# Spreading modulation rows over the partitions with TensorE products, and moving small loads from ScalarE's queue to GpSimd's

## The chip, the cores and the metric

The kernel runs on one core of a Trainium2 chip. The metric is the device time of one execution in microseconds (us), the median over several runs; lower is better. A profile is one further execution, seen by the hardware profiler. In its rows PE is TensorE's matmul, PEld its weight load, DVE is VectorE, ACT is ScalarE, POOL is GpSimd, and SP is the sync engine, which does nothing here but issue DMAs. A name with a q behind it (ACTq, SPq) is the queue side of the engine: the issuing of a DMA, or a wait.

## The reference, cut to what matters

Two networks run one after the other on a sequence of 256 tokens of width 1024. The first has two layers, with a second stream of 256 context tokens (needed in layer 0 only). A layer takes six modulation vectors from a conditioning vector and uses two of them as gates on its two outputs:

```
mod = s_c @ ada_w[l] + ada_b[l]
sh1, sc1, g1, sh2, sc2, g2 = split(mod, 6)
hx = rms_norm(x, norm1_g[l]) * (1.0 + sc1) + sh1
y  = token_mixers(hx, ...) @ w_out          # four mixers: gating, Fourier, two attentions
x  = x + g1 * y
x  = x + g2 * expert_choice_ffn(rms_norm(x, norm2_g[l]) * (1.0 + sc2) + sh2, ...)   # 16 experts
```

`g1` and `g2` are one number for each of the 1024 columns, the same for all tokens. The context stream has its own modulation from the same weights. The second network has two layers of two recurrent mixers, a projection and a feed-forward part; the change doesn't touch its code.

## The kernel before

Tokens lie on the partitions (two tiles of 128 for a stream), the 1024 columns along the free axis. The kernel is written as a Python program whose order is not the order that runs: a scheduler simulates the program at build time and puts each engine's instructions in a fixed list, which the engine then works off strictly in order. An instruction that waits holds up all behind it on its engine. A DMA stands in the list of the engine that issues it.

In order of time, for each of the two layers of the first network:

- `Mods.one` works out a third of the modulation in eight steps: each step loads 1 MB of `ada_w` (SP) and multiplies it in (`pada`, L182). Before the first step the tile `ab` is zeroed on GpSimd (L169) and two loads put the bias `ada_b` into it (L171); after the last, DVE adds it (L187), which gives a row tile, `mrow`. A row tile has 128 partitions, of which eight carry something: partition 32j holds columns 512j to 512j+511 of the token stream's slice, partition 32j+1 the context stream's. Steps that aren't yet needed are put between other work.
- `G1.params` loads one tile of parameters (`pr`, L221) and one of gains (`gn`, L227), a small exponential (`lls`, L234) is made from the latter, and a transpose (`pp`, L223) from the former. In layer 0 it stands in the middle of the first eight modulation steps; the loads for layer 1 are issued in layer 0.
- `G1.hx` norms the tokens: sums of squares (`xn`, L272 on DVE and L274 on ACT), a short chain on DVE, a scaling (L291), transposes on PE (`pt`, L296), and modulation and split into a high and a low part (`hf`, `hT`, L298 to L301).
- The mixers: products with `w_in` (`tokgemm`; its weights `w` come by SP and are split into `whl` by ACT, L62, and DVE, L63; three products for each, L316 to L318), attention units (`psc`, `e`, `wT`), Fourier (`pf`), gating. `bias` is the table of the neighbourhood attention, loaded for each unit by SP.
- `merge` and `project`: the four outputs times `w_out`, times the gate `g1` (DVE, `wtmp`), added to x. The multiplication needs `g1` on all 128 partitions: `g1b`. Here a DMA on SP's queue reads the one partition of `mrow` that holds the row and writes it to 128 (L600): four such copies in layer 0, two in layer 1. The scheduler is free to issue them as soon as `mrow` exists.
- `moe`: `g2` is spread in the same way (L920, four copies to 32 partitions in layer 0, two to 64 in layer 1), then the router, and 16 experts' units whose weights (12 MB for an expert) come by SP in pieces of 1 MB.

PSUM tiles of `moe` and `project` come from pools that take the place of the mixers' pools. The pool `E.m` has one buffer during the mixers and four during `project` and `moe`.

Of the kernel before, what the change touches and what calls it, by code (L numbers as in the profile page):

```python
# [7 lines left out]
FT = mybir.dt.float32  # L8
FR = mybir.dt.float32r
I32 = mybir.dt.int32  # L10
AF = mybir.ActivationFunctionType
# [55 lines left out]
def pairs(r):  # L67

    return slice(256 * (r // 2) + r % 2, 256 * (r // 2) + 256, 2)
# [47 lines left out]
def raw(E, src, kn, st=False):  # L117

    pool, tag = (E.st, "st") if st else (E.wp, "w")
    w = pool.tile([128, kn, src.shape[1]], FT, name="w", tag=tag)  # L120
    E.nc.sync.dma_start(w, src.rearrange("(k p) n -> p k n", p=128))
    return w
# [13 lines left out]
class Mods:  # L136
# [28 lines left out]
    def one(self, l, r, k):  # L165
        E, nc, C = self.E, self.E.nc, self.E.c2
        if k == 0:
            self.ab = E.md.tile([128, 512], FT, name="ab", bufs=1)
            nc.gpsimd.memset(self.ab, 0.0)  # L169
            for s in range(2):  # L170
                nc.scalar.dma_start(self.ab[s:128:32], E.i["ada_b"][l, 2048 * r:2048 * r + 2048].rearrange("(j n) -> j n", j=4))  # L171
            self.ps = E.ad.tile([128, 512], FT, name="pada", tag="ada")
        src = E.i["ada_w"][l, 128 * k:128 * k + 128, 2048 * r:2048 * r + 2048]

        if (l, r) == (0, 0) and k < 3:
            w = E.hl.tile([128, 2048], FT, name="w", tag="whl")
            nc.sync.dma_start(w, src)
        else:
            w = raw(E, src, 1, (l, r) == (0, 0) and k < 7)[:, 0]
        ws = [w[:, 512 * j:512 * j + 512] for j in range(4)]  # L180
        for j in range(4):
            nc.tensor.matmul(self.ps[32 * j:32 * j + 32], self.st[:, k], ws[j],  # L182
                             start=(k == 0), stop=(k == KC - 1), skip_group_check=True)
        if k < KC - 1:
            return
        row = E.md.tile([128, 512], FT, name="mrow", bufs=2) if r else self.ab
        nc.vector.tensor_add(row, self.ps, self.ab)  # L187
        self.row[l, r] = row
        pt = E.m.tile([128, 4, 128], FT, name="pmt", tag="m")
        for q in range(4):  # L190

            nc.tensor.transpose(pt[:, q], row[:, pairs(q) if r else slice(128 * q, 128 * q + 128)], C.id)
        mt = E.md.tile([128, 4, 4, 2], FT, name=f"mt{r}", bufs=2)
        for s in range(2):
            nc.vector.tensor_copy(mt[:, :, :, s], pt[:, :, s:128:32].rearrange("p q j -> p j q"))
        self.T[l, r] = mt
# [7 lines left out]
class G1:  # L204
# [13 lines left out]
    def params(self):  # L218
        E, l, nc, C = self.E, self.l, self.E.nc, self.E.c2
        pr = E.md.tile([32, 128], FT, name="pr1", bufs=1)  # L220
        nc.scalar.dma_start(pr, E.i["par1"][l])  # L221
        pp = E.m.tile([128, 32], FT, name="pp1", tag="m")
        nc.tensor.transpose(pp, pr, C.id[0:32, 0:32])  # L223
        self.pc = E.md.tile([128, 32], FT, name="pc1", bufs=2)
        nc.vector.tensor_copy(self.pc, pp)
        g = E.md.tile([128, 256], FT, name="gn1", bufs=1)
        nc.scalar.dma_start(g, E.i["gains1"][l].unsqueeze(0).to_broadcast([128, 256]))  # L227

        lf = g[:, 128:256].rearrange("p (a b d) -> p a b d", a=2, b=2)
        pd = E.md.tile([128, 2, 32], FT, name="lpd", bufs=1)  # L230
        nc.vector.tensor_mul(pd, lf[:, :, 0], lf[:, :, 1])
        ls = E.md.tile([128, 2], FT, name="lls", bufs=1)
        nc.vector.tensor_reduce(ls, pd, axis=AX.X, op=OP.add)
        nc.scalar.activation(ls, ls, AF.Exp)  # L234
        self.nlam = E.md.tile([128, 1], FT, name="nlam", bufs=2)
        nc.vector.scalar_tensor_tensor(self.nlam, ls[:, 1:2], -self.lam_init, ls[:, 0:1], op0=OP.add, op1=OP.subtract)
        self.gdq = E.md.tile([128, 1], FT, name="gdq", bufs=2)
        nc.vector.tensor_scalar(self.gdq, self.pc[:, 30:31], 0.125, None, op0=OP.mult)
        self.g = g
# [333 lines left out]
    def merge(self):  # L573
# [6 lines left out]
        for k in self.ks:  # L580
# [4 lines left out]
            for s in range(nt // 2):  # L585
                p = pt[:, 256 * s:256 * s + 256]
                nc.scalar.activation(yT[2 * s][:, k], p, AF.Copy, scale=g)
                nc.vector.scalar_tensor_tensor(yT[2 * s + 1][:, k], p, g, yT[2 * s][:, k], op0=OP.mult, op1=OP.subtract)

    def project(self):  # L590

        E, nc = self.E, self.E.nc
        nt, yT = self.nt, self.yT

        row = self.mods.row[self.l, 1]
        W = E.i["w_out"][self.l]
        for c in range(2):
            gb = E.u.tile([128, 2, 512], FT, name="g1b", tag="r4", bufs=3)
            for s in range(nt // 2):
                nc.sync.dma_start(gb[:, s], row[32 * c + s:32 * c + s + 1].unsqueeze(1).to_broadcast([1, 128, 512]))  # L600
            for d in range(2):
                cols = slice(512 * c + 256 * d, 512 * c + 256 * d + 256)

                def ev(s, ps):
                    tmp = E.u.tile([128, 2, 256], FT, name="wtmp", tag="f2", bufs=5)
                    nc.vector.tensor_mul(tmp, ps, gb[:, s, 256 * d:256 * d + 256].unsqueeze(1).to_broadcast([128, 2, 256]))
                    xv = self.X[s][:, :, cols]
                    nc.vector.tensor_add(xv, xv, tmp)
                self.tokgemm(W[:, cols], yT, range(nt // 2), ev, None if c or d else self.ks)
# [65 lines left out]
    def route(self, Q):  # L675
# [90 lines left out]
        me = E.md.tile([48, 32], FT, name="me", bufs=1)[:nr]  # L766
        nc.vector.tensor_scalar(me, m8, thr, None, op0=OP.is_equal)
        nc.vector.tensor_tensor_scan(Wk, one, eq, 0.0, op0=OP.mult, op1=OP.add)
        rem = E.md.tile([48, 1], FT, name="rem", bufs=1)[:nr]
        nc.vector.tensor_reduce(rem, me, axis=AX.X, op=OP.add)  # L770
        nc.vector.scalar_tensor_tensor(eq, Wk, rem, eq, op0=OP.is_le, op1=OP.mult)
        nc.vector.scalar_tensor_tensor(sel, A, thr, eq, op0=OP.is_gt, op1=OP.add)
        nc.vector.tensor_tensor_scan(Wk, one, sel, 0.0, op0=OP.mult, op1=OP.add)
        nc.vector.tensor_mul(Wk, Wk, sel)
        ps = E.m.tile([128, 2, 64], FT, name="psl", tag="m")
# [125 lines left out]
    def moe(self, nxt):  # L901
        E, nc, l = self.E, self.E.nc, self.l
        pool = E.tc.tile_pool
        self.nxk, nwx = (5, 5) if self.last else (8, 3)
        E.turn, E.order = -1, RINGS[self.last]
        with pool(name=f"moe{l}", bufs=1) as Q, pool(name=f"wx{l}", bufs=nwx) as E.wx, \
                pool(name=f"qa{l}", bufs=2, space=PSUM) as E.at, pool(name=f"qm{l}", bufs=4, space=PSUM) as E.m:
            self.early = {}
            if self.last:

                w = self.X[1]
                nc.sync.dma_start(w, E.i["exp_w_gate"][l, 1, 0:256].rearrange("(p k) n -> p k n", k=2))
                self.early["exp_w_gate", 1, 0] = (w[:, 0], w[:, 1])
            self.project()

            self.g2 = E.u.tile([128, 512], FT, name="g2", tag="r4", bufs=3)
            n = 64 if self.last else 32
            for m in range(0, 128, n):
                q = 32 * (2 + m // 64) + (m // 32) % 2
                nc.sync.dma_start(self.g2[m:m + n], self.mods.row[l, 2][q:q + 1].unsqueeze(1).to_broadcast([1, n, 512]))  # L920

            for n, k2 in EARLY[self.last]:
                v = [Q.tile([128, 1024], FT, name="w", tag="xk", bufs=self.nxk) for _ in range(2)]
                for i in range(2):
                    nc.sync.dma_start(v[i], E.i[n][l, 0, 256 * k2 + i:256 * k2 + 256:2])
                self.early[n, 0, k2] = v
            self.route(Q)
            if nxt:
                nxt.params()
                nxt.tables()  # L930
            self.gather(Q, 0, range(2))
            nu = 8 if self.last else 16
            for u in range(nu):
                self.unit(Q, u, None if u else lambda k2: k2 < 3 and self.gather(Q, 0, range(2 * k2 + 2, 2 * k2 + 4)))
                if u < nu // 4:
                    n = 4 * KC // nu
                    self.gather(Q, 1, range(n * u, n * u + n))
# [884 lines left out]
```

## Time and profile before

| | |
|---|---|
| median of 3 runs | 2866.86 us (2862.03 to 2870.46) |
| the profiled execution's own time | 2865.66 us |
| its span in the profile | 2863.9 us |
| PE busy | 2524.6 us, 88% of the span |
| PEld / DVE / ACT / POOL busy | 61% / 48% / 28% / 7% |
| mean granted TensorE clock | 0.947 of full speed |
| moved by DMA | 667.70 MB, a mean of 233 GB/s |

Busy shares are means over stages with different limits. PE looks busy almost throughout because its matmuls are pipelined and their ends are modelled; what matters is where it stands still, and which wait ends last there.

### The profile page before, as it was taken

To read this page: it belongs to the slowest core of one execution; us is meant where nothing else is said; L and a number is where in the kernel's file an instruction comes from. 1 tells how busy PE (TensorE), PEld (TensorE's weight loads), DVE (VectorE), ACT (ScalarE), POOL (GpSimd) and SP (SyncE) were. 2 spreads that over 40 slices of the span, in tenths; PEclk is the share of its full clock that TensorE was granted. 3 is DMA by queue.
4 is the path that set the end of the run, shared out by engine and by line. 5 is a ranking of instruction groups with operands and counts; after the bars stand their busy time and mean duration, and the time that the engine had idled before them with its cause. 6 is when DMAs were issued, how large, how long until landed. Compare 5 with 4: busy or idle time off the path is not lost.

```text
span 2863.9 us, 42312 instructions
## 1 busy us (share of the span) xinstructions
PE 2524.6 (88%) x17723; PEld 1741.9 (61%) x17723; DVE 1369.9 (48%) x2663; ACT 815.6 (28%) x1331; POOL 210.9 (7%) x238
## 2 busy tenths in 40 slices
PE   5979989988889997766667999999998999999898
PEld 3756943322227762111114988888997988879896
DVE  4535643323227653001102767456655777556765
ACT  2324321000003431000002434334443543334442
POOL 0000020000000001000000122000101031100100
PEclk8989999999999999989988998999999998999999
DMA  7566349999995669999997531335553531336453
GB/s 288 177 96 184 140 193 421 421 421 421 421 417 205 151 202 378 421 421 421 421 421 274 161 99 53 111 112 170 191 187 127 162 104 60 104 97 198 161 186 124
DMA packets 238611, 667.70 MB, mean 233 GB/s; under 512 B 11476, under 2 KB 166052, under 8 KB 183508
## 3 DMA queue, kind: packets, MB, share of 16 engines
q1 hardware_dynamic: 236644, 659.91, 63.2%
q0 software_dynamic: 1152, 4.19, 0.5%
q8 instruction: 139, 2.28, 0.3%
q10 hardware_dynamic: 624, 0.89, 0.1%
q14 instruction: 52, 0.43, 0.0%
HBM read 661.78 MB, written 1.05 MB: 231 GB/s over the span
## 4 chain that ended last, share of the span: by engine, by line
PE 65%; DMA 26%; DVE 7%; issue 1%; ACT 1%; POOL 0%; SPq 0%; DVEq 0%; ACTq 0%; POOLq 0%
DMA w<-in_exp_w_up 8%; DMA w<-in_exp_w_down 8%; PE acc L84 8%; PE acc L86 8%; PE acc L85 8%; DMA w<-in_exp_w_gate 6%; PE pj L318 3%; PE pj L316 3%; PE pj L317 3%; PE pgate L852 3%; PE pd L852 2%; PE pup L852 2%; PE dn L1534 2%; PE dn L1532 2%; PE dn L1533 2%; PE pada L182 1%
## 5 line engine op out<-in xcount | busy, mean ns | idle before, releaser
L63 DVE TENSOR_TENSOR whl<-w,whl 128x1024 fp32r<-128x1024 f32 x376 | 464.5, 1238 | 322.5 <-ACT whl L62 321.6
L62 ACT ACTIVATE whl<-w 128x1024 fp32r<-128x1024 f32 x376 | 396.2, 1058 | 492.9 <-PE acc L86 233.1
L84 PE MATMUL acc<-xh,whl 128*128 128x256 f32 x1664 | 475.9, 286 | 0.0
L86 PE MATMUL acc<-xh,whl 128*128 128x256 f32 x1664 | 472.2, 284 | 0.2
L85 PE MATMUL acc<-xl,whl 128*128 128x256 f32 x1664 | 471.0, 283 | 0.0
L84 PEld LDWEIGHTS acc<-xh,whl 128*128 128x128 f32 x1664 | 316.7, 190 | 10.1 <-issue 6.4
L86 PEld LDWEIGHTS acc<-xh,whl 128*128 128x128 f32 x1664 | 316.3, 190 | 5.7 <-issue 3.6
L85 PEld LDWEIGHTS acc<-xl,whl 128*128 128x128 f32 x1664 | 316.5, 190 | 3.6 <-issue 2.8
L852 PE MATMUL pup<-w,xg 128*64 128x512 f32 (+1 forms) x1024 | 223.0, 661 | 69.8 <-DMA w<-in_exp_w_up 69.8
L852 PE MATMUL pd<-w,ehT 128*64 128x512 f32 (+1 forms) x1024 | 205.8, 636 | 56.8 <-DMA w<-in_exp_w_down 39.7
L852 PE MATMUL pgate<-w,xg 128*64 128x512 f32 (+1 forms) x1016 | 215.6, 640 | 45.2 <-DMA w<-in_exp_w_gate 42.6
L852 PEld LDWEIGHTS pup<-w,xg 128*64 128x64 f32 (+1 forms) x1024 | 52.0, 129 | 232.1 <-DMA w<-in_exp_w_up 154.3
L852 PEld LDWEIGHTS pd<-w,ehT 128*64 128x64 f32 (+1 forms) x1024 | 51.8, 127 | 186.9 <-DMA w<-in_exp_w_down 86.6
L852 PEld LDWEIGHTS pgate<-w,xg 128*64 128x64 f32 (+1 forms) x1016 | 50.4, 127 | 175.6 <-DMA w<-in_exp_w_gate 90.0
L316 PE MATMUL pj<-whl,hT 128*128 128x256 f32 x496 | 144.6, 292 | 4.1 <-ACT hT L300 4.1
L318 PE MATMUL pj<-whl,hT 128*128 128x256 f32 x496 | 144.3, 291 | 1.7 <-DVE hT L301 1.7
L317 PE MATMUL pj<-whl,hT 128*128 128x256 f32 x496 | 143.2, 289 | 0.0
L883 DVE TENSOR_TENSOR od<-pd,g 128x512 f32<-128x512 f32 x24 | 16.6, 691 | 232.6 <-PE pd L852 232.6
L871 DVE SCALAR_TENSOR_TENSOR et<-et,pup 128x512 f32<-128x512 f32 x24 | 16.5, 686 | 227.7 <-PE pup L852 227.5
L316 PEld LDWEIGHTS pj<-whl,hT 128*128 128x128 f32 x496 | 95.0, 192 | 19.2 <-issue 9.1
L317 PEld LDWEIGHTS pj<-whl,hT 128*128 128x128 f32 x496 | 95.0, 192 | 11.9 <-issue 8.0
L318 PEld LDWEIGHTS pj<-whl,hT 128*128 128x128 f32 x496 | 95.0, 192 | 11.7 <-issue 8.7
(597 smaller groups left out, 4144.3 us busy)
## 6 DMA issues: line engine op xcount, KB each, us to landing
w<-in_exp_w_down SPq DMA_DIRECT2D x128, 1024.0 KB, 19.5
w<-in_exp_w_up SPq DMA_DIRECT2D x127, 1024.0 KB, 19.8
w<-in_exp_w_gate SPq DMA_DIRECT2D x125, 1024.0 KB, 19.8
w<-in_w_in SPq DMA_DIRECT2D x82, 1024.0 KB, 5.3
w<-in_ada_w SPq DMA_DIRECT2D x48, 1024.0 KB, 7.0
w<-in_w_ffn_up SPq DMA_DIRECT2D x44, 1024.0 KB, 5.1
w<-in_w_ffn_down SPq DMA_DIRECT2D x22, 1024.0 KB, 4.9
w<-in_w_out SPq DMA_DIRECT2D x16, 1024.0 KB, 5.9
```

Source lines behind the costliest of these rows:

```text
L62: nc.scalar.activation(h, w, AF.Copy)
L63: (engine or nc.vector).tensor_sub(lo, w, h)
L84: nc.tensor.matmul(ps[:, b], h[:, k], xh[:, k], start=(k == 0), stop=False)
L85: nc.tensor.matmul(ps[:, b], h[:, k], xl[:, k], start=False, stop=False)
L86: nc.tensor.matmul(ps[:, b], lo[:, k], xh[:, k], start=False, stop=(k == KC - 1))
L316: nc.tensor.matmul(ps, xh, wh, start=start, stop=False, skip_group_check=bool(ks))
L317: nc.tensor.matmul(ps, xh, wl, start=False, stop=False, skip_group_check=bool(ks))
L318: nc.tensor.matmul(ps, xl, wh, start=False, stop=stop, skip_group_check=bool(ks))
L852: m = nc.tensor.matmul(ps[64 * h + mw * i:64 * h + mw * i + mw], lhs(kk, i, e), ws[i][k][:, 512 * h:512 * h + 512], start=(kk == 0), stop= ...
L1532: nc.tensor.matmul(ps[t][g], sh[:, kk, ts], h[:, gs], start=(kk == 0), stop=False)
L1533: nc.tensor.matmul(ps[t][g], sh[:, kk, ts], lo[:, gs], start=False, stop=False)
L1534: return nc.tensor.matmul(ps[t][g], sl[:, kk, ts], h[:, gs], start=False, stop=(kk == nk - 1))
```

## The change

A row is spread by TensorE: a column of the identity matrix, repeated over the output's partitions, is the stationary operand and picks the row q out of the row tile; the result in PSUM has that row on all partitions of the output, and ACT copies it to SBUF. For `g1b` that is one product of 128 partitions for each tile; for `g2`, four products of 32 partitions (layer 0) or two of 64 (layer 1) into one tile. The twelve SP copies go. The loads of `ada_b`, `par1` and `gains1` are issued by GpSimd.

```
-                nc.scalar.dma_start(self.ab[s:128:32], E.i["ada_b"][l, 2048 * r:2048 * r + 2048].rearrange("(j n) -> j n", j=4))
+                nc.gpsimd.dma_start(self.ab[s:128:32], E.i["ada_b"][l, 2048 * r:2048 * r + 2048].rearrange("(j n) -> j n", j=4))
...
-        nc.scalar.dma_start(pr, E.i["par1"][l])
+        nc.gpsimd.dma_start(pr, E.i["par1"][l])
...
-        nc.scalar.dma_start(g, E.i["gains1"][l].unsqueeze(0).to_broadcast([128, 256]))
+        nc.gpsimd.dma_start(g, E.i["gains1"][l].unsqueeze(0).to_broadcast([128, 256]))
...
+    def spread(self, dst, row, qs):
+
+        E, nc = self.E, self.E.nc
+        ps = E.m.tile([128, 512], FT, name="psr", tag="m")
+        n = 128 // len(qs)
+        for i, q in enumerate(qs):
+            nc.tensor.matmul(ps[n * i:n * i + n], E.c2.id[:, q:q + 1].to_broadcast([128, n]), row,
+                             start=True, stop=True, skip_group_check=True)
+        nc.scalar.activation(dst, ps, AF.Copy)
...
-                nc.sync.dma_start(gb[:, s], row[32 * c + s:32 * c + s + 1].unsqueeze(1).to_broadcast([1, 128, 512]))
+                self.spread(gb[:, s], row, [32 * c + s])
...
-            n = 64 if self.last else 32
-            for m in range(0, 128, n):
-                q = 32 * (2 + m // 64) + (m // 32) % 2
-                nc.sync.dma_start(self.g2[m:m + n], self.mods.row[l, 2][q:q + 1].unsqueeze(1).to_broadcast([1, n, 512]))
+            self.spread(self.g2, self.mods.row[l, 2], [32 * (2 + h) + s for h in range(2) for s in range(self.nt // 2)])
```

Since the scheduler sets the order, the change also moves instructions. Three places follow, each as a piece of the difference between the two lists of an engine (a line with - stands only before, one with + only after; `x2` is two in a row).

ACT's list at the start of the program, from its first instruction on. `ab`, `pr` and `gn` are the loads of `ada_b`, `par1` and `gains1`; the second `pr` is layer 1's.

```order
 L149 ACT_TABLE_LOAD
 L149 ACTIVATE crt<-cr 16x128
-L171 DMA ab<-in_ada_b 4x512
-L221 DMA pr_137<-in_par 32x128
 L234 ACTIVATE lls<-lls 128x2
-L221 DMA pr_3330<-in_par 32x128
 L274 ACTIVATE xn,ss_212<-x 128x1024
 L62 ACTIVATE whl<-w 128x1024 x2
```

No DMA stands ahead of the sum of squares (L274) any more; the loads stand on GpSimd's list, behind the zeroing of `ab`.

SP's list in the middle of layer 0's mixers. `w` is a piece of the weights named behind the arrow, `g_3121` is `g2`.

```order
 L121 DMA w<-in_w_in 128x8x256 x2
 L121 DMA w<-in_ada_w 128x2048 x2
-L600 DMA g1b<-mrow 128x1x512 x4
-L121 DMA w<-in_w_in 128x8x256 x2
-L121 DMA w<-in_ada_w 128x2048 x2
-L920 DMA g_3121<-mrow 32x1x512 x4
-L121 DMA w<-in_ada_w 128x2048 x6
+L121 DMA w<-in_w_in 128x8x256 x2
+L121 DMA w<-in_ada_w 128x2048 x8
+L121 DMA w<-in_w_out 128x8x256
```

The weights keep their order, and the copies ahead of them are gone.

PE's list at the end of layer 0's first `project` product (`yT` is the merged mixer output, `mrow` a row tile).

```order
 L316 MATMUL pj<-whl,yT_2577 128x256
 L317 MATMUL pj<-whl,yT_2577 128x256
+L596 MATMUL psr<-mrow,cst_98 128x512 x2
 L318 MATMUL pj<-whl,yT_2578 128x256
 L316 MATMUL pj<-whl,yT_2577 128x256
 L317 MATMUL pj<-whl,yT_2577 128x256
 L318 MATMUL pj<-whl,yT_2578 128x256
+L596 MATMUL psr<-mrow,cst_98 128x512 x2
+L596 MATMUL psr<-mrow,cst_98 32x512 x4
 L316 MATMUL pj<-whl,yT_2575 128x256
```

All eight products of layer 0 stand together there; the copies that SP issued in the middle of the mixers have become work at their end. Besides these places, the lists of PE differ in the second half of layer 0's mixers, at a few places of layer 1's, and in one stretch of the second network's last mixers; the rest reads alike.

## Rows read from the trace of the kernel before

**Rows 1.** The page's chain of work that ended last, shares by engine.

```profile
PE 65%; DMA 26%; DVE 7%; issue 1%; ACT 1%; POOL 0%; SPq 0%; DVEq 0%; ACTq 0%; POOLq 0%
```

**Rows 2.** Stretches: from:to, length, busy PE, PEld, DVE, ACT, POOL, clock, DMA share, GB/s.

```profile
179.00:199.00 20.00, 0.00 (x0) 0.00 (x0) 0.07 (x1) 1.16 (x2) 0.00 (x0) 0.53 0.91 123
199.00:204.00 5.00, 4.78 (x18) 4.01 (x19) 3.73 (x9) 1.24 (x5) 0.00 (x0) 0.50 0.02 6
204.00:317.00 113.00, 112.68 (x750) 83.15 (x750) 68.00 (x207) 52.19 (x123) 1.05 (x2) 1.00 0.42 123
357.00:405.00 48.00, 38.57 (x179) 20.69 (x179) 27.95 (x63) 13.54 (x21) 17.91 (x14) 0.89 0.24 88
405.00:855.00 450.00, 403.15 (x1896) 139.99 (x1892) 133.86 (x212) 34.91 (x57) 8.82 (x24) 1.00 1.01 420
1021.00:1031.00 10.00, 9.80 (x28) 5.52 (x29) 1.70 (x4) 1.45 (x4) 0.00 (x0) 0.54 0.22 73
2270.00:2450.00 180.00, 177.79 (x1776) 153.52 (x1776) 134.15 (x320) 74.17 (x144) 46.73 (x50) 0.94 0.28 86
```

**Rows 3.** Timeline of ACT, 0 to 62 us: start, duration, instruction, idle before.

```profile
27.61 0.33 ACTq L221 DMA_DIRECT2D pr<-in_par  x1
27.99 1.06 ACT L274 ACTIVATE xn<-x 128x1024 f32<-128x1024 f32 x1 [22.37 <-DMA w<-in_ada_w]
...
30.62 2.00 ACT L62 ACTIVATE whl<-w 128x1024 fp32r<-128x1024 f32 x2 [1.49 <-DMA w<-in_w_in]
41.22 0.56 ACT L298 ACTIVATE hf<-pt,mt,aff 128x256 f32<-128x256 f32 x1 [8.59 <-DVE aff L258]
```

**Rows 4.** Timeline of DVE, same stretch.

```profile
17.53 1.22 DVE L272 SCALAR_TENSOR_TENSOR xn<-x 128x1024 f32<-128x1024 f32 x1 [4.76 <-DMA x<-in_x]
...
39.22 0.69 DVE L187 TENSOR_TENSOR ab<-pada,ab 128x512 f32<-128x512 f32 x1 [6.46 <-issue]
```

**Rows 5.** Timeline of PE, same stretch.

```profile
32.15 3.68 PE L296 MATMUL pt<-cst,xn 128*128 128x128 f32 x16 [10.18 <-DVE xn L291]
35.75 3.33 PE L182 MATMUL pada<-w,cst 128*32 128x512 f32 x24
```

**Rows 6.** Timeline of SP's queue, 145 to 235 us.

```profile
149.81 2.48 SPq L600 DMA_DIRECT2D g1b<-mrow  x4
169.25 17.39 SPq L121 DMA_DIRECT2D w<-in_w_in  x2
```

**Rows 7.** DMA issues of the whole span: count, size of one, median us to landing.

```profile
w<-in_w_in SPq DMA_DIRECT2D x82, 1024.0 KB, 5.3
...
gb<-in_ln_gb POOLq DMA_DIRECT2D x8, 512.0 KB, 4.9
bias<-in_na_bias SPq DMA_DIRECT2D x8, 256.0 KB, 3.0
...
g1b<-mrow SPq DMA_DIRECT2D x6, 256.0 KB, 25.6
```

**Rows 8.** Timeline of ACT, 165 to 205 us.

```profile
197.84 1.06 ACT L62 ACTIVATE whl<-w 128x1024 fp32r<-128x1024 f32 x1 [26.01 <-DMA w<-in_w_in]
```

**Rows 9.** Timeline of PE, 174 to 200 us.

```profile
199.22 1.12 PE L435 MATMUL psc<-cv,wT 128*128 128x64 f32 x4 [20.36 <-ACT wT L428]
```

**Rows 10.** Timeline of SP's queue, 840 to 1115 us.

```profile
1006.79 2.26 SPq L920 DMA_DIRECT2D g<-mrow  x2
...
1010.92 0.35 SPq L476 DMA_DIRECT2D bias<-in_na_bias  x1
```

**Rows 11.** Timeline of PE, 1004 to 1034 us.

```profile
1021.20 1.19 PE L484 MATMUL psc<-bias,cst 128*128 128x256 f32 x2 [3.81 <-DMA bias<-in_na_bias]
```

**Rows 12.** The chain, 0 to 1000 us: start, duration, instructions (two rows a product).

```profile
223.88 1.72 PE pf L510 x4
...
239.88 1.00 PE pada L182 x8
```

**Rows 13.** Instructions on tile bz (ACT's copy from PSUM), ns min/median/max.

```profile
L361 ACT ACTIVATE bz<-pj x3: 591/598/609, 204.0 to 935.2; 128x512 f32<-128x512 f32 x3
```

## Prediction

> **What bounds the kernel now.** I read the chain of work that ended last first. It is mostly PE, with a quarter of the span on DMA [rows 1]; DVE has 7%, ACT and GpSimd next to nothing. So an edit pays only where it lets PE go on sooner, or lets weights come sooner in the stretches that weights bound. I then cut the span into stretches [rows 2]. From 405 to 855 us (layer 0's experts) the DMA engines are full, at 420 GB/s: that stretch is as long as its bytes take. In the mixers, 204 to 317 us, PE is busy 112.68 of 113 us at full clock. Between these two kinds lie a few places where PE stands still, and the change touches three of them: the program's start, 179 to 204 us, and 1010 to 1031 us. I looked up each in the timelines and asked which wait ended last.
>
> *The start.* ACT's first large instruction, the sum of squares L274, begins at 27.99 us after 22.37 us of idleness [rows 3]. Its input was there at 17.53 us: DVE's L272 reads the same tokens then [rows 4]. What stands ahead of it in ACT's list is the second `par1` load (L221), issued at 27.61 us, and what released that is a piece of `ada_w`. So a load for layer 1 holds up ACT by ten, and PE's transposes come at 32.15 us, after 10.18 us of waiting [rows 5].
>
> *Layer 0.* Four `g1b` copies are issued at 149.81 us [rows 6], long before their use. One lands after 25.6 us, though it is a quarter the size of a `w_in` piece, which takes 5.3 us [rows 7]. While they run, the DMA engines are busy 0.91 of the time in a stretch that moves 123 GB/s in the mean [rows 2]. The `w_in` piece issued behind them at 169.25 us ends a wait of 26.0 us on ACT, and through ACT one of 20.4 us on PE [rows 8, 9]. When PE comes back it has the lower clock: 0.50 of full speed, that is 1.2 of 2.4 GHz, from 199 to 204 us [rows 2].
>
> *Layer 1.* The `g2` copies go out at 1006.79 us, and a `bias` table behind them at 1010.92 us [rows 10]; PE waits 3.81 us for that table, until 1021.20 us [rows 11], and then runs ten microseconds at a granted clock of 0.54 [rows 2].
>
> **The change part by part.** The sum is made against the profiled execution's 2865.66 us, which lies 1.2 us below the median, 2866.86 us.
>
> *Loads off ACT's list.* L274 can start at 17.6 us. In the trace PE's transposes start 32.15 - 27.99 = 4.2 us after it, so at 21.8 us, and take 3.6 us, to 25.4. The last three `ada_w` steps then cost 3.33 / 3 = 1.1 us each [rows 5], but the last piece lands only at 27.6 us (it is what released the load on ACT), so they end at 28.7 us, and DVE's addition comes at 28.8 instead of 39.22 us [rows 4]: 10.4 us gained. Next in line is the `w_in` split on ACT (L62): its piece landed at 30.62 us, it takes 2.00 us, and it stands ahead of the modulation L298, which so starts at 32.6 instead of 41.22 us [rows 3]. That leaves **8.6 us**. The ends for the range are 10.4 and nothing. Nothing would come if the GpSimd loads were late; the only such load in the trace, 512 KB, lands in 4.9 us [rows 7], and the first addition needs `ab` some 25 us after its zeroing. The later `ada_b` loads move from ACT to a GpSimd that is mostly idle; I cost them at nothing. On GpSimd's list the second `par1` load again waits, for PE's transpose of the first; behind it are only a zeroing and the rope tables, which nobody wants before the keys are projected.
>
> The Trainium skill speaks against this gain: by "DMA: Bandwidth & Descriptors" (Issuing engines are not separate DMA queues) loads issued from another engine still share the DMA engines, and only the time to issue them is saved. By that rule the term would be 0 and the sum 2843 us. The row on L274 says otherwise here, because what goes is not the issuing but the wait in front of it in an in-order list.
>
> *Layer 0's `g1b` copies off SP.* The weights keep their order. The `w_in` piece of 169.25 us should land 5.3 us later, at 174.6. ACT had been waiting for it since 197.8 - 26.0 = 171.8 us [rows 8] and would split it by 175.6; PE ran dry at 199.2 - 20.4 = 178.8 us [rows 9]. The margin is 3 us, so the whole 20.4 us goes, and with it the slow restart: half of the 4.78 us that PE works at half clock [rows 2], 2.4 us. Together **22.8 us**; the lower end, if a third of the wait came back as another, is 15. The four `g2` copies of layer 0 lie beside a PE that never stops (204 to 317 us), so their going is worth nothing.
>
> *Layer 1.* Its two `g1b` copies also lie beside a busy PE. Without the `g2` copies the `bias` table should land 3.0 us after its issue [rows 7], at 1013.9 us, before PE's need at 1021.20 - 3.81 = 1017.4. Gained are the 3.8 us and the slow clock behind it, 9.80 x 0.46 = 4.5 us: 8.3 at most, nothing at least. I take **8.0**.
>
> *What is added.* A product of 128x512 costs two rows of `pf`, 1.72 / 2 = 0.86 us; four products of 32 columns cost 1.00 us as in `pada` [rows 12]. Layer 0: 4 x 0.86 + 1.0 = 4.4 us. Layer 1: 2 x 0.86, and two products of 64 columns, between 0.5 (half of the four) and 1.7 (as two whole ones), taken as 0.9: 2.6 us. They stand in `project`, where PE is the bound: **7.0 us** on the path. ACT's eight copies of 0.6 us [rows 13] lie beside these products and the next; without that cover they would cost up to 4.8 us. A wait for the PSUM bank that the mixers give back isn't in the trace; the products stand near the end of the list of the first `w_out` product, so I take 0, with 2 as the upper end.
>
> *The moved order.* PE had 0.3 us of idleness in 204 to 317 us, so a new order can't gain there and can lose. In the other stretch with a new order, 2270 to 2450 us, it is idle 2.2 of 180 us [rows 2]; a like share of 113 us is 1.4. I take **1.0**, up to 5.
>
> *Does an earlier mixer end pass through the experts?* Between 357 and 405 us the DMA engines are busy 0.24 of the time [rows 2]: expert weights wait for buffers, that is for the program, and the full stretch begins when it gets there. The bytes behind are the same, so it ends earlier by as much.
>
> Sum: -8.6 - 22.8 - 8.0 + 7.0 + 1.0 = -31.4; 2865.7 - 31.4 = **2834 us**.
>
> **The rivals.** *The start gives nothing*: something else holds up the sum of squares or the first addition until 28 us and more. For it: three of the loads that the first microseconds need now come from GpSimd, one after the other. Against it: 25 us of slack. Time: 2834 + 8.6 = 2843 us.
>
> *New waits take part of it*: layer 1's clock still falls because PE is thin there anyway, or the new order of layer 0's mixers leaves holes, or `project` waits for ACT's copies. For it: the order changed where PE was tight. Time: from 2842 (layer 1's 8 lost) over 2851 (with the start's 8.6) to 2856 (with 5 for order).
>
> *No change*: the copies were a symptom and the weights come late anyway, for instance because buffers free late. Against it: the `w_in` piece needs 28.6 us behind the copies and 5.3 elsewhere. Time: 2866 + 7 - 8.6 = 2864 us.
>
> *Slower*: a GpSimd load of `ada_b` comes so late that DVE's addition L187 waits for it, with DVE's whole list behind, and so the first transposes of the modulation and all of layer 0. At the start each microsecond after 28.8 us costs one. It decides for slower by over 0.3% (2875.5 us) only if the first load lands after 28.8 + 41 = 70 us, fourteen times the 4.9 us in the trace. Time there: 2876 us.
> The Trainium skill has the mechanism: by "SBUF — State Buffer" (SBUF: two separate sides), GpSimd can't write the descriptors of its DMAs while DVE runs an instruction that takes both ports. No run here shows it yet; DVE stands idle for 4.76 us ahead of its first large instruction [rows 4], so by that rule too the loads would be in time.
>
> **How the numbers follow.** 0.3% (8.6 us) is about what a measurement of this kernel can tell from no change. Chances: the forecast 0.62, with a range of its own from 2828 (all upper ends, 2831, and a little for what the copies cost elsewhere) to 2841; the start gives nothing 0.12 (2843); new waits 0.14 (2842 to 2856); no change 0.06; slower 0.06. The first three are faster by over 0.3%: 0.88. The range from 2824 to 2856 holds them and leaves out 0.12.
>
> **What would show it.** In the profile after: ACT's L274 at about 17.6 us and L298 at 32 to 34; no gap of PE near 170 us (the old 179, less the start's gain) and no stretch with a DMA share of 0.91 at 123 GB/s; the `psr` products at 4.4 us in layer 0's `project`; PE not waiting for `bias` in layer 1; layer 0's experts ending near 829 instead of 855 us. The prediction is wrong if L274 still starts late, if PE's gap in the mixers stays above 8 us, or if the experts' full stretch ends when it did.

## The result, and the profile after

| | before | after |
|---|---|---|
| median | 2868.66 us (4 runs, 2862.03 to 2874.96) | 2838.77 us (4 runs, 2837.20 to 2843.52) |
| the profiled execution's own time | 2865.66 us | 2838.47 us |
| its span | 2863.9 us | 2836.7 us |
| mean granted TensorE clock | 0.947 | 0.956 |

The ratio of the times is 0.9899, with a 95% interval from 0.9873 to 0.9925: faster by 1.0%, or 29 us (the medians differ by 29.9). The forecast was 2834 us with a range from 2824 to 2856.

I read the profile after at the places where the prediction had read the one before. The timeline of ACT at the start, which answers to [rows 3]:

```profile
19.87 1.06 ACT L274 ACTIVATE xn<-x 128x1024 f32<-128x1024 f32 x1 [11.50 <-DMA x<-in_x]
...
32.94 2.00 ACT L62 ACTIVATE whl<-w 128x1024 fp32r<-128x1024 f32 x2 [11.92 <-DMA w<-in_w_in]
34.85 1.91 ACT L298 ACTIVATE hf<-pt,mt,aff 128x256 f32<-128x256 f32 x4
```

No load stands ahead of the sum of squares any more; it now waits for its own input. But that input comes at 19.87 us instead of 17.53, and the `w_in` piece at 32.94 instead of 30.62. The modulation (L298) starts 6.4 us sooner, where 8.6 was forecast.

In layer 0, the piece of `w_in` in question on SP's queue, and then its split on ACT; they answer to [rows 6] and [rows 8]:

```profile
160.27 3.04 SPq L121 DMA_DIRECT2D w<-in_w_in  x2
```

```profile
165.52 1.06 ACT L62 ACTIVATE whl<-w 128x1024 fp32r<-128x1024 f32 x1 [2.67 <-DMA w<-in_w_in]
```

From issue to use it is now 5.2 us instead of 28.6, and ACT's wait is 2.67 us instead of 26.01. The stretches, with the columns of [rows 2]:

```profile
160.00:200.00 40.00, 40.00 (x270) 31.53 (x269) 18.45 (x53) 15.19 (x38) 1.64 (x3) 1.00 0.31 106
...
394.00:827.00 433.00, 388.45 (x1822) 134.12 (x1818) 131.48 (x208) 32.71 (x53) 8.82 (x24) 1.00 1.01 421
990.00:1000.00 10.00, 10.00 (x62) 6.91 (x60) 5.35 (x19) 5.51 (x12) 0.00 (x0) 1.00 0.11 36
```

PE doesn't stop once between 160 and 200 us, at full clock. The experts' full stretch is as full as before and lies earlier: in pieces of 5 us the DMA share falls below 1 at 830 us (0.79 from 830 to 835) where it fell at 860 (0.36 from 860 to 865). The place in layer 1 where PE waited for `bias` and then ran at 0.54 is now busy at 1.00. PE's timeline there has the product with `bias` without a wait, and the added products cost what their rows say:

```profile
290.70 1.88 PE L596 MATMUL psr<-mrow,cst 128*128 128x512 f32 x4
292.89 2.87 PE L596 MATMUL psr<-mrow,cst 128*128 128x512 f32 x12
...
989.97 0.60 PE L484 MATMUL psc<-bias,cst 128*128 128x256 f32 x2
...
1018.60 1.02 PE L596 MATMUL psr<-mrow,cst 128*128 128x512 f32 x2
...
1022.90 2.03 PE L596 MATMUL psr<-mrow,cst 128*128 128x512 f32 x6
```

That is 4.75 us in layer 0 and 3.05 in layer 1 (two rows for a product). A new wait came with them, DVE's for ACT's copies, in the view of the tile `psr` (who waited for it: us, times):

```profile
  DVE wtmp L616: 4.3, 2
```

To see where the time went I set the PE instructions of the two traces beside each other in order and took how much earlier each one starts after the change (the median over 8 us about a moment of the kernel before). The last column is the same for a second profiled execution of the changed kernel, from the experiments below:

```
us of before   after, first   after, second   what lies between
     110          -6.4           -5.9         the start
     178          -9.0           -4.1         (clock, see the last section)
     205         -31.8          -27.0         the gap behind the g1b copies
     317         -30.9          -26.0         new order of layer 0's mixers
     335         -26.3          -21.4         products of layer 0
    1010         -26.9          -20.0         layer 0's experts
    1041         -35.1          -28.3         the wait for bias and its slow clock
    1060         -32.2          -25.3         products of layer 1
    2400         -29.6          -25.2         experts, second network
    2600         -27.5          -23.0         new order of the last mixers
    2800         -27.0          -22.3
```

The change between 110 and 178 us is no work of the edit: the kernel before had a clock of 0.66 from 125 to 130 us, the first execution after it had full clock there, and the second was slower than both.

### The profile page after: what moved, and what is told of

Same layout as the page of the kernel before. It is cut to its first block, busy times and chain, and to the rows that moved or that the text cites. A ratio compares the mean times of both kernels' runs of the same rounds, so it can differ in the third digit from the quotient of the medians.

```text
span 2836.7 us, 42367 instructions
## 1 busy us (share of the span) xinstructions
PE 2525.5 (89%) x17747; PEld 1743.9 (61%) x17747; DVE 1371.0 (48%) x2663; ACT 819.0 (29%) x1339; POOL 217.0 (8%) x254
## 3 DMA queue, kind: packets, MB, share of 16 engines
q8 instruction: 139, 2.28, 0.3%
## 4 chain that ended last, share of the span: by engine, by line
PE 66%; DMA 25%; DVE 6%; ACT 1%; issue 1%; POOL 0%; SPq 0%; DVEq 0%; ACTq 0%; POOLq 0%
DMA w<-in_exp_w_down 9%; DMA w<-in_exp_w_up 8%; PE acc L84 8%; PE acc L86 8%; PE acc L85 8%; DMA w<-in_exp_w_gate 6%; PE pj L316 3%; PE pj L318 3%; PE pj L317 3%; PE pgate L862 3%; PE pd L862 2%; PE pup L862 2%; PE dn L1541 2%; PE dn L1540 2%; PE dn L1539 2%; PE pada L182 2%
## 5 line engine op out<-in xcount | busy, mean ns | idle before, releaser
L317 PEld LDWEIGHTS pj<-whl,hT 128*128 128x128 f32 x496 | 94.1, 190 | 12.3 <-issue 8.9
```

What stands on the lines that cost most here:

```text
L317: nc.tensor.matmul(ps, xh, wl, start=False, stop=False, skip_group_check=bool(ks))
```

## The experiments

The theory after the result is that of the prediction: three waits went, each with its own cause (`par1` on ACT's list; the `g1b` copies in layer 0; the `g2` copies in layer 1), and the products and a new order of PE's list take a little back. Three things were open: whether the parts stand alone, why the start gave less, and whether a copy is slow because of its queue, its shape or its source. Ratios are to the kernel before on the same chip, with 95% intervals. The edits are shown shortened.

**One part at a time.**

```
e2: kernel before, and nc.scalar -> nc.gpsimd for ada_b, par1, gains1
e3: kernel before, and nc.scalar -> nc.gpsimd for par1 alone
e4: kernel before, and for layer 1 alone
-   nc.sync.dma_start(self.g2[m:m + n], self.mods.row[l, 2][q:q + 1].unsqueeze(1).to_broadcast([1, n, 512]))
+   self.spread(self.g2, self.mods.row[l, 2], [64, 96])
e12: kernel before, and for layer 0 alone
-   nc.sync.dma_start(gb[:, s], row[32 * c + s:32 * c + s + 1].unsqueeze(1).to_broadcast([1, 128, 512]))
+   self.spread(gb[:, s], row, [32 * c + s])
```

Expected of the loads alone (e2):

> The kernel before with only the loads of ada_b, par1 and gains1 moved to GpSimd; all twelve copies stay on SP. Main theory: ACT's sum of squares starts near 20 us, the first product with w_in comes 6 us sooner, the copies are issued 6 us sooner too, and the gap of 20 us behind them stays as long: 2869 - 6 = 2863 us. Rival A (caught up later): the gap ends at the same time as before, near 199 us, so nothing is gained: 2869 us. Rival B (part of the big gain is the loads'): the gap shrinks below 10 us, 2850 us.

Measured: 2862.92 us against 2869.96, ratio 0.9976 (0.9964 to 0.9988). PE's gap was 19.6 us long and ended at 192.97 us instead of 199.22:

```profile
192.97 1.12 PE L435 MATMUL psc<-cv,wT 128*128 128x64 f32 x4 [19.60 <-ACT wT L428]
```

So the start's gain is passed through whole; both rivals fall.

Of `par1` alone (e3), whose PE, DVE and SP lists are those of the kernel before:

> The kernel before with only the two loads of par1 moved to GpSimd; ada_b, gains1 and all twelve copies stay where they were, and the lists of PE, DVE and SP are the same. Main theory (of the moved loads only layer 1's par1, which stands ahead of the sum of squares and waits, costs anything): ACT's sum of squares starts near 17.6 us, the modulation near 32.6 (8.6 sooner), and the time is 2870 - 8 = 2862 us. Rival A (the ada_b loads on ACT's list hold the start as well): modulation later than 36 us, 2866 us or more. Rival B (the second par1 load was only the one that showed): sum of squares stays near 28 us, 2870 us.

Measured: 2859.07 us against 2867.85, ratio 0.9970 (0.9960 to 0.9981). ACT's timeline:

```profile
17.57 1.06 ACT L274 ACTIVATE xn<-x 128x1024 f32<-128x1024 f32 x1 [12.39 <-DMA x<-in_x]
...
32.56 1.00 ACT L298 ACTIVATE hf<-pt,mt,aff 128x256 f32<-128x256 f32 x2
```

The sum of squares starts at its forecast time, and the modulation 8.66 us sooner than in [rows 3], which is the 8.6 of the prediction. So of the three loads `par1` alone held up the start; that it was layer 1's is read from [rows 3], since e3 moved both.

Of layer 1's `g2` copies alone (e4):

> The kernel before with only layer 1's two g2 copies turned into products (64 partitions each); the four g1b and four g2 copies of layer 0, the two g1b copies of layer 1 and all loads stay as before. Main theory: the wait of 3.8 us for the bias table in layer 1 and the ten microseconds at half clock behind it are gone (7 us), the products cost 1: 2869 - 6 = 2863 us. Rival (layer 1's gain came from its g1b copies, or from the earlier stages ending sooner): the wait for bias stays at 2 us or more and the clock there stays near 0.54; 2868 to 2870 us.

Measured: 2863.08 us against 2869.96, ratio 0.9973 (0.9963 to 0.9983). The wait for `bias` is gone although layer 1's `g1b` copies are still there; the rival falls. PE's products with `bias` stand without one, for instance

```profile
1013.42 0.65 PE L484 MATMUL psc<-bias,cst 128*128 128x256 f32 x2
```

Of layer 0's `g1b` copies alone (e12):

> The kernel before with only layer 0's four g1b copies turned into products; the loads stay on ACT, and the g2 copies of both layers and layer 1's g1b copies stay on SP. By itself the scheduler now issues layer 0's four g2 copies later, among the first weights of the experts. Main theory: PE's gap of 20.4 us and the slow restart behind it are gone (23 us), the four products cost 3.4, the wait for bias in layer 1 stays at 3.7 us; the g2 copies, 128 packets of about 1.09 us, hold the 16 engines for 8.7 us just where the weights set the pace, which costs up to that: 2866 - 23 + 3.4 = 2846 us without that cost and 2855 with it. Rival (half of the gap was due to something else in layer 0, the g2 copies or the loads on ACT): a gap of 8 us or more stays, 2857 us and more.

Measured: 2850.33 us against 2869.67, ratio 0.9934 (0.9914 to 0.9954). PE has no gap in layer 0's mixers, and still waits 3.79 us for `bias` in layer 1:

```profile
1005.47 1.19 PE L484 MATMUL psc<-bias,cst 128*128 128x256 f32 x2 [3.79 <-DMA bias<-in_na_bias]
```

The four `g2` copies, now issued at 300.57 us ahead of expert weights, cost about 2.2 us there (PE's lead over the kernel before, taken as in the table above, falls from 17.4 us at 365 us to 15.2 at 400), less than the 8.7 that were possible:

```profile
300.57 4.47 SPq L933 DMA_DIRECT2D g<-mrow  x4
317.16 0.33 SPq L132 DMA_DIRECT2D w<-in_exp_w_up  x1
```

**Half of the suspected cost (e9).** Two of layer 0's four `g1b` copies back in the changed kernel:

```
+   if c == 0 and not self.last:
+       nc.sync.dma_start(gb[:, s], row[s:s + 1].unsqueeze(1).to_broadcast([1, 128, 512]))
+       continue
    self.spread(gb[:, s], row, [32 * c + s])
```

> The changed kernel with two of layer 0's four g1b copies (the first half of the columns) back on SP, and their two products gone; nothing else is put back. Theory 1 (the gap is the time that the copies' packets hold the engines, 128 x 1.09 / 16 = 8.7 us for a copy, less what PE has in store): with two copies instead of four the gap shrinks from 20.4 to about 3 us: 2839 + 3 + 1 - 2 = 2841 us. Theory 2 (any copy there delays the weights, whatever the number): a gap of 15 us or more, 2855 us. Theory 3 (PE has more in store than thought): no gap, 2837 us.

Measured: 2837.74 us, ratio 0.9898 (0.9884 to 0.9912). ACT's timeline, and the stretch of 165 to 180 us:

```profile
173.40 1.06 ACT L62 ACTIVATE whl<-w 128x1024 fp32r<-128x1024 f32 x1 [6.91 <-DMA w<-in_w_in]
```

```profile
165.00:180.00 15.00, 13.74 (x81) 10.33 (x80) 7.53 (x25) 4.32 (x12) 0.00 (x0) 0.83 0.59 147
```

ACT waits 6.9 us where it waited 26.0 behind four copies and 2.7 behind none; PE stands still for 1.3 us. So ACT's wait grows with the number of copies, though not in proportion, and most of a short one is covered by what PE has in store. PE's gap lies between the 3 us of theory 1 and none of theory 3, whose times differ by less than the runs scatter; theory 2 falls.

**Queue, shape or source (e7, e5).** Both spread without products: e7 copies from SBUF as before, but on GpSimd's queue; e5 goes through a scratch place in DRAM (`E.dr` is a pool of tiles there).

```
e7: +   nc.gpsimd.dma_start(dst[n * i:n * i + n], row[q:q + 1].unsqueeze(1).to_broadcast([1, n, 512]))
e5: +   d = E.dr.tile([1, 512], FT, name="drow", bufs=12)
    +   nc.gpsimd.dma_start(d, row[q:q + 1])
    +   nc.gpsimd.dma_start(dst[n * i:n * i + n], d[0].unsqueeze(0).to_broadcast([n, 512]))
```

> The changed kernel with no products for the spread: the twelve copies from SBUF as in the kernel before, but issued by GpSimd instead of SP. Theory 1 (the copies hold the 16 DMA engines, which all queues share): packets of 2 KB near 1.09 us again, the w_in piece waits as before, PE's gap of 15 to 20 us in layer 0 is back: 2839 - 7 + 20 + 5 = 2857 us. Theory 2 (the copies delayed the weights only because they stood ahead of them on SP's queue): no gap, and the products' 7 us are saved: 2832 us.

Measured (e7): 2859.67 us, ratio 0.9979 (0.9971 to 0.9988). The gap on PE moved forward with the copies, and a wait for `bias` is back (PE's timeline):

```profile
123.14 0.79 PE L316 MATMUL pj<-whl,hT 128*128 128x256 f32 x2 [8.68 <-ACT whl L62]
...
1014.60 0.77 PE L484 MATMUL psc<-bias,cst 128*128 128x256 f32 x2 [3.66 <-DMA bias<-in_na_bias]
```

So copies that GpSimd issues hold up weights on SP's queue, which is theory 1; its sizes were off. The gap is 8.7 us instead of 15 to 20: here the four copies leave in two pairs, at 106.78 and 134.55 us, and PE stands still only behind the first (a clock of 0.62 from 115 to 125 us and 0.50 to 130 goes with it; in all PE falls back by 11.3 us). Layer 1 costs more than was expected: PE falls back by 10 us between 925 and 1010 us. That the time is so near the 2857 expected is in part luck.

> The changed kernel with no products for the spread: GpSimd writes each row (2 KB) to a scratch place in DRAM, and a second DMA on GpSimd's queue reads it from there to all partitions. The same bytes land on the same partitions as by the twelve copies of the kernel before. Theory 1 (the copies were slow because 128 packets all read one partition of SBUF; 2 KB took 1.09 us each): packets from DRAM take 0.1 us or so, no stretch of full DMA engines, no gap of PE in layer 0, and the products' 7 us are saved: 2839 - 6 = 2833 us. Theory 2 (the copies were slow because 128 rows of 2 KB are written from one row, whatever the source): packets near 1 us again, a gap of 10 us and more in layer 0, 2850 to 2865 us.

Measured (e5): 2832.13 us, ratio 0.9886 (0.9873 to 0.9898). The median is 6.6 us under the changed kernel's, but the two ratios, each to its own runs of the kernel before, are only 0.13% apart and their intervals overlap. The trace is clearer: PE's lead over the kernel before is 26.7 us at 317 and at 335 us, and 35.0 us at 1041 and at 1060, so it loses nothing at the two places where the products cost 4.6 and 2.9. Its DMA issues, with the columns of [rows 7]:

```profile
g1b<-drow POOLq DMA_DIRECT2D x6, 256.0 KB, 5.0
...
g<-drow POOLq DMA_DIRECT2D x4, 64.0 KB, 2.2
...
drow<-mrow POOLq DMA_DIRECT2D x12, 2.0 KB, 5.0
```

The same 256 KB land in 5.0 us from DRAM and in 25.6 from one partition of SBUF [rows 7], where four were issued together (12.3 for two together, in e7). The packets in the traces say it without this waiting for each other:

```
copies from           by       packets      one (median)
one SBUF partition    SP       512 x 2 KB   1.088 us   (before, 140 to 210 us)
one SBUF partition    GpSimd   320 x 4 KB   2.278 us   (e7, 100 to 300 us)
DRAM                  GpSimd   320 x 4 KB   0.173 us   (e5, 100 to 300 us)
128 SBUF partitions   SP       512 x 2 KB   0.086 us   (before, x to DRAM at the end)
```

So neither the queue nor the shape makes a copy slow, but its source: some thirteen times as long for the same packet on the same queue. The last row, the store of the result, says that it isn't SBUF as a source either, but one partition for all packets (it writes to DRAM, but e5's packets write to SBUF and aren't slow). Sixteen engines with 2 KB in 1.09 us each make 30 GB/s, with 4 KB in 2.28 us 29 GB/s: by this estimate the time goes with the bytes and not with the number of packets. Theory 1 holds in both, theory 2 falls in both.

**The loads put back (e1), and `gains1` alone (e6).**

```
e1: changed kernel, nc.gpsimd -> nc.scalar for ada_b, par1, gains1
e6: changed kernel, nc.gpsimd -> nc.scalar for gains1 alone
```

> The changed kernel with its loads of ada_b, par1 and gains1 back on ACT's list; the products stay. Main theory (three separate gains: 6.4 us at the start from the loads, 23 in layer 0 from the g1b copies, 7 in layer 1 from the g2 copies): ACT's sum of squares starts near 28 us again, the gap of PE in layer 0's mixers stays away, and the time is that of the changed kernel plus 6.4, so about 2845 us, 23 under the kernel before. Rival A (the start's gain is caught up later, because the weights of the mixers come no sooner): the first product with w_in is 6 us later, but layer 0's mixers end where they end in the changed kernel, 2839 us. Rival B (the gap in layer 0 went because the start moved, not because the copies went): the gap of 20 us is back, 2865 us.

Measured (e1): 2854.92 us, ratio 0.9949 (0.9937 to 0.9960). The sum of squares is at 27.77 us again and the gap stays away, as expected, but the time is 10 us above the main theory's. Some 8 of them are lost in layer 1's mixers, which I had not thought of: set beside the changed kernel's first execution, PE lies 11 us behind when they begin and 19 when they end (4 and 12 beside its second). Nearly the same work on PE (stretches, e1 first, then the changed kernel):

```profile
914.00:1029.00 115.00, 110.34 (x659) 73.28 (x657) 64.62 (x189) 49.11 (x97) 0.52 (x1) 0.96 0.41 136
```

```profile
905.00:1008.00 103.00, 102.03 (x649) 69.98 (x648) 62.55 (x185) 47.37 (x92) 1.66 (x3) 1.00 0.45 151
```

With the loads back the scheduler wrote another order; it leaves PE idle for 4.7 us instead of 1.0 there, and the clock falls for a while. That the order is the cause wasn't tested by itself.

> The changed kernel with only the two loads of gains1 back on ACT's list, ahead of everything there; ada_b and par1 stay on GpSimd. In the changed kernel the tokens x land at 19.87 us and in the kernel before at 17.53. Theory 1: the gains load takes longer on the DMA engines when GpSimd issues it (32 packets of 0.99 us, where ACT's had 128 of 0.05) and that is what delays x and the w_in piece behind it; then the sum of squares starts near 17.6 us and the modulation near 32.6: 2839 - 2.2 = 2837 us. Theory 2: x is late because SP issues it in another place or for chance; then the sum of squares stays at 19.5 to 20.5 us and the time at 2839.

Measured (e6): 2839.84 us, ratio 0.9886 (0.9870 to 0.9901). ACT's timeline:

```profile
17.51 1.06 ACT L274 ACTIVATE xn<-x 128x1024 f32<-128x1024 f32 x1 [12.59 <-DMA x<-in_x]
...
32.59 1.92 ACT L298 ACTIVATE hf<-pt,mt,aff 128x256 f32<-128x256 f32 x4
```

The start is what theory 1 says, 2.3 us sooner: the `gains1` load, not chance, delays x. The time doesn't show it; it runs from 2832.26 to 2843.12 us, so 2.3 us can't be told there.

**Once more, and put together (e10, e8, e11).** The changed kernel again; rows through DRAM with `gains1` on ACT; and that with `ada_b` on ACT too.

> The changed kernel once more, nothing edited, so that the two kernels beside it can be set against it on one chip. All theories: 2837 to 2843 us, and the sum of squares near 20 us again, if the late landing of x comes from GpSimd's load of gains1 and not from chance.

> Rows spread through DRAM by GpSimd (no products), and the two loads of gains1 back on ACT's list; ada_b and par1 stay on GpSimd. Theory 1 (the two gains add up, 6.6 us from the products and 2.3 from the start): 2839 - 9 = 2830 us, with the sum of squares at 17.5 us. Theory 2 (what the start gains is lost again in the later stages, as the time with gains1 on ACT and the products kept, 2840 us, suggests): 2832 to 2833 us.

> Rows spread through DRAM by GpSimd, par1 loaded by GpSimd, but gains1 and ada_b both on ACT's list as in the kernel before. Theory 1 (ada_b on ACT costs nothing that matters): as with ada_b on GpSimd, 2830 us. Theory 2 (the ada_b loads on ACT change the order in layer 1 for the worse, as in the run with the products and all loads on ACT, where the end of layer 1's mixers cost 10 us): 2838 to 2842 us.

Measured, on one chip: 2840.36 us (ratio 0.9909, 0.9892 to 0.9925), 2833.87 us (0.9882, 0.9864 to 0.9901) and 2828.20 us (0.9867, 0.9851 to 0.9882). The sum of squares of the repeat is at 20.05 us, as expected. e8 lies 6.5 us under the repeat, though the intervals overlap and it also has `gains1` back on ACT; against e6, which has that too, its ratio differs by 0.04% only. So what rows through DRAM save in time isn't told closely by these runs. e11's interval lies clear of the repeat's. With `gains1` moved back, e8 is no faster than e5, so its theory 2 fits better. e11 is near the 2830 us of its theory 1, but that theory set it equal to e8, and it came out 6 us lower (their intervals overlap). In the two profiled executions these 6 us lie in the second network, far from the loads: about 3 near 1600 us of the kernel before, where the clock of e8 is 0.91 (1520 to 1560 us of its own time) and that of e11 1.00, and the rest between 1780 and 1900, where the order of e11's list differs. So I don't put it down to `ada_b`. It is the fastest kernel here: of the three loads only `par1` moved, and no product at all.

## Why the prediction held, point by point

The time lies 5 us above the forecast, and inside the forecast case's own range. By its steps:

- **Loads off ACT's list: 8.6 forecast, 6.4 measured.** The wait and its owner were right (e3). The step that was off is the condition that the input comes at 17.53 us: moving `gains1` costs 2.3 us of it (e6). I had costed the other moved loads at nothing.
- **Layer 0: 22.8 forecast, 22.8 and 22.9 measured** between 178 and 205 us in the two executions, the slow restart included. Alone, this part with its products is worth 19 us (e12).
- **Layer 1: 8.0 forecast, 8.2 and 8.3 measured**, and it is the `g2` copies (e4).
- **Products: 7.0 forecast, 7.5 measured** on PE's path, 4.6 in layer 0 (317 to 335 us) and 2.9 in layer 1 (1041 to 1060); their rows make 7.8. DVE's wait of 4.3 us for ACT's copies doesn't show on PE.
- **The moved order: 1.0 forecast, 3.0 measured:** 0.9 us between 205 and 317 us, and 2.1 to 2.2 between 2400 and 2600. Between 205 and 317 us e2, which has no products, loses the same 0.9, and e1, e11 and e12, which have `ada_b` on ACT's list, 0.1 at most, so that part goes with moving `ada_b`. Between 2400 and 2600 us the eleven traces with the new order of the last mixers lose 1.3 to 2.3 us, and the two without it (e3, e4) 0.2 at most. It is inside the 5 that were allowed.
- **The pass through the experts** held: from 335 to 1010 us PE's lead changes by 0.6 us in one execution and 1.4 in the other.

The terms as measured make -6.4 - 22.8 + 0.9 + 4.6 - 8.2 + 2.9 + 2.1 = -26.9, against -31.4. The difference of 4.5 is 2.2 at the start, 2.0 in the order and 0.5 in the products, less 0.2 gained in layer 1. The spans differ by 27.2, but that the sum comes so near is in part luck: what it leaves out (the clock between 110 and 178 us, smaller changes later) cancels in this execution. In the second one the same terms make -26.3, and the spans differ by 22.6.

Of the rivals, that the start gives nothing fell with e2 and e3, and that nothing changes fell with the result. *New waits* had the order at 5 us and layer 1's 8 us as lost; the order took 3.0, and layer 1's clock was 1.00. Slower through late GpSimd loads fell: DVE's first addition started at 31.08 us and waited for PE, not for `ab`. It is 2.3 us later than the 28.8 of the prediction, as the tokens are.

```profile
31.08 0.69 DVE L187 TENSOR_TENSOR ab<-pada,ab 128x512 f32<-128x512 f32 x1 [1.59 <-PE pada L182]
```

The Trainium skill, "DMA: Bandwidth & Descriptors" (Issuing engines are not separate DMA queues), has it that DMAs run on the same 16 DMA engines whichever engine issues them, and that issuing from several engines saves only the time of issuing. The trace of e7 agrees with the first half: copies on GpSimd's queue held up weights on SP's. The second half leaves out what e3 shows: there the move of two loads of 16 KB is worth 8.8 us, because an instruction of an in-order list had been waiting in front of work.

## What to carry to other kernels

Look in an engine's list for the small DMA that waits: what it costs is the work queued behind it, not its bytes. Price a DMA by how long it holds the DMA engines, and read that from its packets: here 128 of 1.09 us on 16 engines, 8.7 us for 256 KB, where 1 MB of weights landed in 5.3. A landing time far above that of others of its size, 25.6 us here, is the sign to look, but it holds the waiting behind others as well. When a slow operation is replaced by work on the engine that sets the end, look for a third way that uses neither: here a detour through DRAM took no time on PE, and the fastest kernel used it.

## What the runs showed of the hardware

A DMA that reads one SBUF partition for all its packets took 1.09 us for 2 KB issued by SP, and 2.28 us for 4 KB issued by GpSimd, and held the DMA engines meanwhile (a share of 0.91 at 123 GB/s [rows 2]); from DRAM 4 KB took 0.17 us, and from 128 partitions of SBUF 2 KB took 0.09.

A load of `gains1` (128 KB, one row to 128 partitions, from DRAM) took 128 packets with a median of 0.05 us when ACT issued it and 32 of 0.99 us when GpSimd did, 12.2 and 29.7 us in sum. Later GpSimd loads of the same kind of packet took 0.17 us (e5), so it isn't the queue alone; what else it was stays open.

The clock differs between executions of one program. The stretch of 112 to 122 us, first in the changed kernel's first profiled execution, then in its second:

```profile
112.00:122.00 10.00, 9.65 (x50) 5.08 (x49) 6.91 (x14) 5.43 (x10) 0.00 (x0) 1.00 0.83 307
```

```profile
112.00:122.00 10.00, 9.68 (x30) 5.00 (x33) 5.93 (x12) 5.43 (x11) 0.00 (x0) 0.61 0.80 296
```

PE is as busy in both, but the clock granted is 1.00 in one and 0.61 in the other. For the same instructions the second execution is 0.6 us behind the first at 112 us and 4.9 at 120, so 4.3 us are lost there. A sum that spans such a stretch can't be told more closely than that from one trace.
